# Ten of 22 feature tiles of each FFN for both token halves together, in seven block products for eight

## The chip, the cores and the metric
One core of a Trainium2 chip. The metric is device time in microseconds, the median of some runs. The engines named below are TensorE (PE, with its weight loads as PEld), VectorE (DVE), ScalarE (ACT), GpSimd (POOL) and SyncE (SP), which only issues transfers here.

## What is computed
A block of 1024 tokens of width 1024, all fp32 in and out. The reference, cut to its frame:

```python
x = x + 0.5 * _swiglu(_rms_norm(x, ffn1_norm), ffn1_w_gate, ffn1_w_up, ffn1_w_down)
h = _rms_norm(x, mix_norm)
proj = h @ w_in
...
mixed = concatenate([o_gla, o_rwkv])       # two recurrent mixers over chunks of tokens
x = x + mixed @ w_out
x = x + 0.5 * _swiglu(_rms_norm(x, ffn2_norm), ffn2_w_gate, ffn2_w_up, ffn2_w_down)
return _rms_norm(x, final_norm)
# _swiglu(h, g, u, d) = (silu(h @ g) * (h @ u)) @ d, with 2816 features between
```

## The kernel before
The tokens are worked in two halves A and B of 512 (`HT`). The 2816 features of an FFN are 22 tiles of 128 (`NF`). Each fp32 product is three products of rounded parts: `mm3` (and its yielding form `mm3y`) multiplies high by high, high by low and low by high parts. A weight tile gets its parts in `stage`: SP loads it (`raw`, `NR` buffers), ACT casts the high part `wH` (L394), DVE subtracts it for the low part `wL` (L395). The normalised tokens are kept as the parts `xnH` and `xnL`.

`ffn` is a generator over one half. Feature tiles go in groups of four; for each tile 48 gate and up products into the banks `pgu`, `silu` on ACT, the product `hf` on DVE, its parts `hH` and `hL`; then for each group 24 down products per tile into `pdn`, which DVE adds to x (L533). Every product is a yield, so that other code can take from the generator as many products as it wants. That is what `mixers` does: between the small steps of a mixer (two GLA units, four RWKV pairs: `rwkv_unit`) it writes FFN products of the other half into TensorE's stream, as many as a table of latencies says (`LAT`, `SLACK`, `FILL`). So B's first FFN (`f1b`) fills A's mixer, and A's second (`f2a`) fills B's. TensorE's stream is in the order in which it is written; the other engines' streams are ordered by a scheduler that also moves work of later code ahead.

An RWKV pair first inverts its triangular blocks of 32 by 63 small DVE operations (L89 to L91, n from high to 1; the transposed result is D, L94), then makes `p`, `pav`, and then goes through 8 chunks in turn: `pz` product, Z on DVE (L147), `pz`, UV by DVE and ACT (L152, L153), `pz`, the new state Xn on DVE (L159), with `py` beside it. A group norm over the pair's output YS (L168 to L177), the transposes `pyT`, and two DVE operations end it (L186 to L190), and `YS` is stored to DRAM as `mix`. `outprep` loads the eight mix tiles and makes `xnH`, `xnL` of them (L940, L941); `outproj` is the output projection (`pout`), which DVE adds to x (L953).

After the mixer the main sequence says how many of the FFN's steps are taken where:

```python
mixers(A, f1b)
...
load_x(A, xsp(A))
outprep(A)
run(f1b, n=3)
outproj(A)
run(f1b)
new_xn(A)
norm(A.x, A.XH, A.XL, "n2")
```

`mixers` itself stops taking products at a label, `last=("gu", 5, 20)`, that is at the gate and up products of tile 20 in the last group; `run(f1b, n=3)` stands over the output projection's preparation, and the last `run(f1b)` over the norm.

## Time and profile before
| | |
|---|---|
| runs | 2159.74, 2160.78, 2161.89 us, median 2160.78 |
| span of the profiled execution | 2160.3 us |
| PE busy | 2138.7 us, 99% of the span |
| DVE busy | 1298.8 us, 60% |
| ACT busy | 894.7 us, 41% |
| POOL busy | 83.2 us, 4% |
| mean granted clock of TensorE | 0.999 |

The profiled execution has nothing around its span that the runs' times show: the median lies 0.5 us above it. Busy times are of one engine, and the engines work beside each other, so their sum is no time. A granted clock of 1.00 is 2.4 GHz and 0.5 is 1.2 GHz.

### The profile page before, as it was taken

How to read it: one execution, taken by the hardware profiler on the slowest of the kernel's cores; microseconds unless marked ns; L12 is line 12 of the kernel's file. 1: busy time of each engine (PE TensorE's matmuls, PEld its weight loads, DVE VectorE, ACT ScalarE, POOL GpSimd, SP SyncE). 2: the span in 40 equal slices, each digit the busy share in tenths (PEclk: the TensorE clock that was granted, in tenths of full speed). 3: DMA queues.
4: the chain of work that ended last, by engine and by line, in shares of the span. 5: the costliest groups of instructions: out<-in, count | busy, mean ns of one | idle time of the engine just before them, and what ended most of it. 6: DMA issues, size and time to landing. Idle time of an engine off the chain costs nothing.

```text
span 2160.3 us, 34594 instructions
## 1 busy us (share of the span) xinstructions
PE 2138.7 (99%) x12924; PEld 1682.7 (78%) x12924; DVE 1298.8 (60%) x3387; ACT 894.7 (41%) x1719; POOL 83.2 (4%) x161
## 2 busy tenths in 40 slices
...
GB/s 197 89 86 98 103 94 97 145 193 188 267 102 94 123 99 90 108 92 176 108 126 198 194 271 93 93 118 103 91 106 91 178 88 142 93 98 97 94 95 76
DMA packets 135064, 269.61 MB, mean 125 GB/s; under 512 B 16080, under 2 KB 18160, under 8 KB 134896
## 3 DMA queue, kind: packets, MB, share of 16 engines
...
## 4 chain that ended last, share of the span: by engine, by line
PE 96%; DVE 2%; DMA 1%; ACT 1%; issue 0%; SPq 0%; ACTq 0%; DVEq 0%
PE pgu L43 45%; PE pdn L43 23%; PE pp L43 11%; PE pout L43 4%; PE pz L43 3%; PE pv L43 2%; PE po L43 1%; PE py L43 1%; PE ptn L46 1%; PE pt L46 1%; PE pB L43 1%; PE pg L43 1%; DMA UV<-d_vt 0%; PE pav L43 0%; PE p L43 0%; DVE lb L89 0%
## 5 line engine op out<-in xcount | busy, mean ns | idle before, releaser
L394 ACT CAST wH<-raw 128x512 fp32r<-128x512 f32 (+2 forms) x670 | 413.2, 620 | 882.1 <-PE pgu L43 367.7
L395 DVE TENSOR_TENSOR wL<-raw,wH 128x512 fp32r<-128x512 f32 (+2 forms) x670 | 458.8, 688 | 472.9 <-ACT wH L394 468.2
L43 PE MATMUL pgu<-xnH,wH 128*128 128x512 f32 (+1 forms) x1424 | 563.8, 397 | 0.0
L43 PE MATMUL pgu<-xnL,wH 128*128 128x512 f32 (+1 forms) x1424 | 563.4, 396 | 0.3 <-DVE xnL L479 0.3
L43 PE MATMUL pgu<-xnH,wL 128*128 128x512 f32 (+1 forms) x1424 | 562.5, 395 | 0.2 <-DVE wL L395 0.2
L43 PEld LDWEIGHTS pgu<-xnL,wH 128*128 128x128 f32 x1424 | 267.5, 188 | 59.4 <-DVE xnL L479 0.7
L43 PEld LDWEIGHTS pgu<-xnH,wL 128*128 128x128 f32 x1424 | 267.3, 188 | 59.3 <-DVE wL L395 0.4
L43 PEld LDWEIGHTS pgu<-xnH,wH 128*128 128x128 f32 x1424 | 267.2, 188 | 58.7
L43 PE MATMUL pdn<-wH,hL 128*128 128x512 f32 x704 | 281.6, 400 | 0.0
L43 PE MATMUL pdn<-wH,hH 128*128 128x512 f32 x704 | 280.0, 398 | 0.0
L43 PE MATMUL pdn<-wL,hH 128*128 128x512 f32 x704 | 279.0, 396 | 0.0
L533 DVE SCALAR_TENSOR_TENSOR x<-pdn,x 128x512 f32<-128x512 f32 x192 | 131.9, 689 | 136.1 <-PE pdn L43 135.3
L43 PEld LDWEIGHTS pdn<-wH,hL 128*128 128x128 f32 x704 | 132.1, 188 | 31.1 <-DVE hL L574 0.4
L43 PEld LDWEIGHTS pdn<-wL,hH 128*128 128x128 f32 x704 | 132.2, 188 | 30.5
L43 PEld LDWEIGHTS pdn<-wH,hH 128*128 128x128 f32 x704 | 132.1, 188 | 29.8 <-ACT hH L573 0.5
L43 PE MATMUL pp<-xnH,wH 128*128 128x512 f32 x352 | 140.4, 399 | 0.0
L43 PE MATMUL pp<-xnH,wL 128*128 128x512 f32 x352 | 138.5, 393 | 0.0
L43 PE MATMUL pp<-xnL,wH 128*128 128x512 f32 x352 | 138.4, 393 | 0.0
L570 DVE TENSOR_TENSOR hf<-pgu,silu 128x512 f32<-128x512 f32 x88 | 60.8, 691 | 95.9 <-PE pgu L43 95.5
L43 PEld LDWEIGHTS pp<-xnH,wL 128*128 128x128 f32 x352 | 66.1, 188 | 15.4
L43 PEld LDWEIGHTS pp<-xnH,wH 128*128 128x128 f32 x352 | 66.1, 188 | 15.1 <-issue 0.7
L43 PEld LDWEIGHTS pp<-xnL,wH 128*128 128x128 f32 x352 | 66.2, 188 | 14.3
...
## 6 DMA issues: line engine op xcount, KB each, us to landing
...
d_x<-x SPq DMA_DIRECT2D x8, 512.0 KB, 2.6
d_AR<-AR POOLq DMA_DIRECT2D x8, 512.0 KB, 4.7
...
```

The source lines that it names most:

```text
L43: return self.t.matmul(out,lhsT,rhs,**kw)
L46: return self.t.transpose(out,in_,idn)
L394: S.copy(H, raw)
L395: V.tensor_tensor(L, raw, H.bitcast(F32), op=SUB)
L533: V.scalar_tensor_tensor(h.x[tt][:, co], ps, 0.5, h.x[tt][:, co], op0=MULT, op1=ADD)
L570: V.tensor_tensor(hf, pgu[1], s, op=MULT)
```

## The change
Tiles 12 to 21 of each FFN (five `PAIRS`) leave the generator and are computed for both halves in blocks of two by two: two feature tiles or two halves of the model width on one side, the two token halves on the other, by Winograd's form of Strassen's product: seven block products for eight, with sums of weight blocks and of token blocks ahead and sums of results behind.

`combine` makes the token sums T1 to T4. `joint_up` goes through the pairs; for gate (m=0) and up (m=1) it makes 7 block products of 12 matmuls (`pju`), with three new weight sums `s1`, `s2`, `s3` and a fourth in place on POOL, sums behind them on DVE, and then `put`s seven combinations of the four hidden blocks, each as high and low part in a tile `hh` of 512 KB (two buffers), to DRAM. `joint_down` goes through the seven products in `ORDER`; for each it goes through the five pairs, loads a combination back (`hh`, five buffers), sums weight blocks on POOL and makes 12 matmuls into four banks (`pjd`); behind each product DVE adds the banks to x of both halves. Half B's normalised tokens go through DRAM (`norm_store`, `from_store`); x of both halves is loaded again behind `joint_up`.

The generators keep twelve tiles, in three groups (`FOURS`), in the first FFN's A half in six (`TWOS`). The label in `mixers` is as before, and no group 5 exists in `FOURS`. `NH, NL, NR` go from 8, 8, 3 to 6, 6, 4. The diff, cut:

```diff
-GROUPS = [[0, 1, 2, 3], [4, 5, 6, 7], [8, 9, 10, 11], [12, 13, 14, 15], [16, 17, 18, 19], [20, 21]]
-GROUPS_LAST = [[0, 1], [2, 3, 4, 5], [6, 7, 8, 9], [10, 11, 12, 13], [14, 15, 16, 17], [18, 19, 20, 21]]
+
+NS = 12
+PAIRS = [(f, f + 1) for f in range(NS, NF, 2)]
+FOURS = [list(range(f, min(f + 4, NS))) for f in range(0, NS, 4)]
+TWOS = [list(range(f, min(f + 2, NS))) for f in range(0, NS, 2)]
+CUT = 6
+
+ORDER = [1, 6, 2, 7, 5, 4, 3]
...
-NH, NL, NR = 8, 8, 3
+NH, NL, NR = 6, 6, 4
...
+    def joint_up(w, X, ep):
+
+        def tmp(nm):
+            return ep.tile([P, HT], F32, tag="e", bufs=11, name=nm)
+
+        def left(f1, f2, m):
+
+            raw = {(i, kh): stage_load(wgu[w][(f * 2 + m) * 2 + kh]) for kh in range(2) for i, f in ((1, f1), (2, f2))}
+            yield 1, stage_f(raw[1, 0])
+            s1 = ep.tile([P, HT], F32, tag="s", bufs=3, name="s1")
+            GP.tensor_tensor(s1, raw[2, 0], raw[2, 1], op=ADD)
+            s2 = ep.tile([P, HT], F32, tag="s", bufs=3, name="s2")
+            GP.tensor_tensor(s2, s1, raw[1, 0], op=SUB)
+            yield 6, stage_f(s2)
+            yield 2, stage_f(raw[1, 1])
+            s3 = ep.tile([P, HT], F32, tag="s", bufs=3, name="s3")
+            GP.tensor_tensor(s3, raw[1, 0], raw[2, 0], op=SUB)
+            yield 7, stage_f(s3)
+            yield 5, stage_f(s1)
+            yield 4, stage_f(raw[2, 1])
+            GP.tensor_tensor(s2, raw[1, 1], s2, op=SUB)
+            yield 3, stage_f(s2)
+
+        for j, (f1, f2) in enumerate(PAIRS):
+            gate = {}
+            for m in range(2):
+                C = {}
+                for i, u in left(f1, f2, m):
+                    ps = pm.tile([P, HT], F32, tag="pm", name="pju") if i in (6, 7, 4) else pa.tile([P, HT], F32, tag="pa", name="pju")
+                    for q in range(4):
+                        sl = slice(P * q, P * q + P)
+                        xo = (X[i][0][:, q], X[i][1][:, q])
+                        mm3(ps, (u[0][:, sl], u[1][:, sl]), xo, q == 0, q == 3)
...
+            def put(op, f):
+                hh = ep.tile([P, 2, HT], F32R, tag="hh", bufs=2, name="hh")
+                halved(f, hh[:, 0], hh[:, 1])
+                nc.gpsimd.dma_start(hid_dram(w, j, op), hh.bitcast(F32).rearrange("p a t->p (a t)"))
+
+            put(1, a11)
+            s1 = tmp("s1")
+            GP.tensor_tensor(s1, a21, a22, op=ADD)
+            s2 = tmp("s2")
+            GP.tensor_tensor(s2, s1, a11, op=SUB)
+            put(6, s2)
+            put(2, a12)
+            GP.tensor_tensor(a11, a11, a21, op=SUB)
+            put(7, a11)
+            put(5, s1)
+            put(4, a22)
+            GP.tensor_tensor(s2, a12, s2, op=SUB)
+            put(3, s2)
...
+        for i in ORDER:
+            ps = banks(int(i in (6, 7, 4)))
+            for j in range(n):
+                u = right(i, j)
+                hh = ep.tile([P, 2, HT], F32R, tag="hh", bufs=5, name="hh")
+                nc.sync.dma_start(hh.bitcast(F32).rearrange("p a t->p (a t)"), hid_dram(w, j, i))
+                for t in range(4):
+                    to = slice(P * t, P * t + P)
+                    mm3(ps[t], (hh[:, 0, to], hh[:, 1, to]), u, j == 0, j == n - 1)
...
+    norm_store(B, "n1")
+    run(f1a, until=("dn", 1, 1))
+    tcm = tc.tile_pool(name="tp", bufs=1, side="right", reuse_waits="tile")
+    tpool = tcm.__enter__()
+    fcm, fpool = extras("left")
+    X = combine(A, B, tpool, fpool)
+    fcm.__exit__(None, None, None)
+    run(f1a)
+    spill(A)
+    hp.close()
+    close_x(A)
+    ecm, ep = extras("left")
+    joint_up(0, X, ep)
+    ecm.__exit__(None, None, None)
+    tcm.__exit__(None, None, None)
+    open_x(A)
+    load_x(A, xsp(A))
+    open_half(B, "right")
     load_x(B, xin(B))
-    new_xn(B)
-    norm(B.x, B.XH, B.XL, "n1")
-    run(f1a)
-    f1b = ffn(B, 0)
+    ecm, ep = extras("left")
+    joint_down(0, A, B, ep)
+    ecm.__exit__(None, None, None)
+    from_store(B)
+    B.stored = False
+    hp = Hid("right", 5)
+    f1b = ffn(B, 0, hp)
     new_xn(A)
...
     run(f2a, n=3)
+    to_store(A)
     outproj(B)
...
+    A.stored = True
+    tcm, tpool = extras("left")
+    fcm, fpool = extras("left")
+    hp = Hid("right", 3)
+    f2b = ffn(B, 1, hp, groups=[[f, f + 1] for f in range(0, CUT, 2)])
+    run(f2b, until=("gu", 0, 1))
+    X = combine(B, A, tpool, fpool)
+    fcm.__exit__(None, None, None)
+    run(f2b)
+    spill(B)
+    hp.close()
+    close_x(B)
+    ecm, ep = extras("left")
+    joint_up(1, X, ep)
+    ecm.__exit__(None, None, None)
+    tcm.__exit__(None, None, None)
+    open_x(B)
+    load_x(B, xsp(B))
+    open_x(A)
+    load_x(A, xsp(A))
+    ecm, ep = extras("left")
+    joint_down(1, B, A, ep)
+    ecm.__exit__(None, None, None)
+    hp = Hid("right", 5)
```

How it moves instructions, by the order of both programs. On PE, in a chunk of the last pair of A's mixer, before (`pgu` is a gate or up product of `f1b`):

```order
L43 MATMUL pz<-Z,R_8997 64x64 x2
L43 MATMUL pgu<-xnH,wL 128x512
L43 MATMUL pgu<-xnH,wH 128x512
L43 MATMUL pgu<-xnL,wH 128x512
L43 MATMUL pgu<-xnH,wL 128x512
L43 MATMUL pgu<-xnH,wH 128x512
L43 MATMUL pgu<-xnL,wH 128x512
L43 MATMUL pgu<-xnH,wL 128x512
L43 MATMUL pgu<-xnH,wH 128x512
L43 MATMUL pgu<-xnL,wH 128x512
L43 MATMUL pz<-UV,WN_9025 64x64
L43 MATMUL pz<-UV,WN_9026 64x64
```

Nine FFN products stand there between the `pz` that takes Z and the `pz` that takes UV. In the changed kernel, some chunks earlier (`pdn` is a down product of `f1b`):

```order
L43 MATMUL pdn<-wH,hL 128x512
L43 MATMUL pdn<-wH,hH 128x512
L43 MATMUL pdn<-wL,hH 128x512
L43 MATMUL pdn<-wH,hL 128x512
L43 MATMUL pz<-Z,R_9714 64x64 x2
L43 MATMUL pz<-UV,WN_9740 64x64
L43 MATMUL pz<-UV,WN_9741 64x64
L43 MATMUL pz<-Xn,AR 64x64 x2
L43 MATMUL py<-Xn,AR 64x64 x2
L43 MATMUL py<-UV,W_8699 64x64
L43 MATMUL py<-UV,W_8700 64x64
```

The four `pdn` rows are the last FFN products of this mixer: the 174 mixer products behind them, this chunk and all later ones, have none between them.

At the end of the mixer, before, on PE (`pyT` are the transposes behind the last group norm):

```order
L43 MATMUL pgu<-xnL,wH 128x512
L43 MATMUL pgu<-xnH,wL 128x512
L43 MATMUL pgu<-xnH,wH 128x512
L46 MATMUL pyT<-ct,YS 128x128 x4
L43 MATMUL pgu<-xnL,wH 128x512
L43 MATMUL pgu<-xnH,wL 128x512
L43 MATMUL pgu<-xnH,wH 128x512
L43 MATMUL pgu<-xnL,wH 128x512
```

and in the changed kernel, there:

```order
L43 MATMUL py<-Xn,AR 64x64 x2
L43 MATMUL py<-UV,W_9938 64x64
L43 MATMUL py<-UV,W_9939 64x64
L46 MATMUL pyT<-ct,YS 128x128 x4
L43 MATMUL pout_10733<-wH,xnH 128x512
L43 MATMUL pout_10733<-wL,xnH 128x512
L43 MATMUL pout_10733<-wH,xnL 128x512
```

Before, 128 FFN products stand between `pyT` and `pout`; now the first `pout` product is the next row.

On SP, where FFN1 goes from `joint_up` to `joint_down` in the changed kernel (`xnL` is B's tokens, `x` half A's, `hh` a combination of hidden blocks, `raw` a weight tile; the waits name a queue or an engine: DMASW is a queue of POOL, DMAHW one of SP):

```order
L662 DMA xnL_4701<-d_xf1_705 128x512 [waits DMAHW6_49]
L548 DMA x_3803<-d_x_0_2083 128x1024 [waits DMAHW7_49,DVE_49]
...
L548 DMA x_3809<-d_x_0_2083 128x1024 [waits DMAHW2_49]
L815 DMA hh_3846<-d_hid0_0_1_2396 128x1024 [waits DMASW5_49,DMASW7_49,DMASW3_49,DMAHW3_49,DMASW1_49,DMASW0_49]
L815 DMA hh_3866<-d_hid0_1_1_2737 128x1024 [waits DMAHW4_49]
...
L815 DMA hh_3926<-d_hid0_4_1_3760 128x1024 [waits DMAHW7_49,DMASW4_49]
L393 DMA raw_3978<-in_wdn1_dram 128x512 [waits DMAHW0_49,Pool_49]
L815 DMA hh_3961<-d_hid0_0_6_2405 128x1024 [waits DMAHW3_49,DMAHW1_49,PE_49]
```

Every load of `joint_down` behind its first weight tiles stands behind the four loads of x, which wait for DVE, and behind the first `hh`, which waits for four of POOL's stores.

On ACT at the same place (`hh` casts are the puts of the last pair; `xnH` casts belong to `from_store`):

```order
L633 CAST hh_3766<-s2_3764 128x512 [waits DMASW3_49,Pool_49]
L633 CAST hh_3771<-u3_3545 128x512 [waits DMASW4_49,DVE_49,Activation_49]
L633 CAST hh_3777<-p1_3482 128x512 [waits DMASW5_49,DVE_49,Pool_49]
L633 CAST xnH_4698<-xnL_4700 128x512 [waits DMAHW7_49,PE_49]
L633 CAST hh_3782<-s1_3762 128x512 [waits DMASW6_49,DVE_49]
L633 CAST xnH_4698<-xnL_4700 128x512 [waits DMAHW0_49]
L633 CAST xnH_4698<-xnL_4700 128x512 [waits DMAHW1_49]
L633 CAST xnH_4698<-xnL_4700 128x512 [waits DMAHW2_49]
L633 CAST xnH_4699<-xnL_4701 128x512 [waits DMAHW3_49]
L633 CAST hh_3787<-c22_3564 128x512 [waits DMASW7_49,DVE_49]
```

The casts of the puts wait in turn for POOL's stores (DMASW), whose tile they take, so that the last ones come after them all.

In FFN2's joint_down the loads on SP stand thus (`x_20290` is half A's, `x_20273` half B's):

```order
L548 DMA x_20290<-d_x_0_2083 128x1024
L815 DMA hh_20313<-d_hid1_0_1_18866 128x1024 [waits DMAHW7_49,DMASW7_49]
...
L815 DMA hh_20393<-d_hid1_4_1_20230 128x1024 [waits DMAHW3_49,DMASW3_49]
L393 DMA raw_20445<-in_wdn2_dram 128x512 [waits DMAHW4_49,Pool_49]
L815 DMA hh_20428<-d_hid1_0_6_18875 128x1024 [waits DMAHW5_49,DMAHW7_49,DMASW0_49,PE_49]
L393 DMA raw_20448<-in_wdn2_dram 128x512 [waits DMAHW6_49]
L815 DMA hh_20455<-d_hid1_1_6_19216 128x1024 [waits DMAHW0_49,DMASW7_49,PE_49]
L548 DMA x_20273<-d_x_1_11334 128x1024 [waits DMASW5_49,DMASW7_49,DMASW1_49,DVE_49]
L548 DMA x_20275<-d_x_1_11334 128x1024 [waits DMAHW1_49]
...
L393 DMA raw_20475<-in_wdn2_dram 128x512 [waits DMAHW6_49]
L815 DMA hh_20482<-d_hid1_2_6_19557 128x1024 [waits DMAHW7_49,PE_49]
```

Here the first `hh` waits for data alone, and half B's x, which waits for stores of POOL and for DVE, stands between the second and the third `hh` of product 6.

## Rows read from the trace of the kernel before

**Rows 1.** The page, parts 1 and 4: TensorE, and the last chain by engine.
```profile
PE 2138.7 (99%) x12924; PEld 1682.7 (78%) x12924; DVE 1298.8 (60%) x3387; ACT 894.7 (41%) x1719; POOL 83.2 (4%) x161
...
PE 96%; DVE 2%; DMA 1%; ACT 1%; issue 0%; SPq 0%; ACTq 0%; DVEq 0%
```

**Rows 2.** The last chain in time: start, length, engine, products of one kind.
```profile
163.43 44.40 PE pgu L43 x192
207.83 22.23 PE pdn L43 x96
```

**Rows 3.** Windows: length, busy us (count) of PE, PEld, DVE, ACT, POOL; clock; DMA; GB/s.
```profile
844.20:986.10 141.90, 141.90 (x848) 105.61 (x845) 77.32 (x226) 49.95 (x107) 0.00 (x0) 1.00 0.33 99
986.10:1015.50 29.40, 29.40 (x129) 23.84 (x128) 17.64 (x28) 13.15 (x24) 0.00 (x0) 1.00 0.64 224
1060.20:1082.30 22.10, 22.10 (x97) 17.64 (x96) 17.34 (x57) 9.26 (x18) 0.00 (x0) 1.00 0.38 137
427.00:432.00 5.00, 5.00 (x27) 4.54 (x27) 1.16 (x2) 4.33 (x8) 3.48 (x7) 0.66 0.91 326
7.00:12.00 5.00, 4.30 (x20) 3.69 (x20) 3.92 (x11) 3.59 (x11) 0.00 (x0) 1.00 0.99 365
```

**Rows 4.** Timeline of DVE (start, us, line, operation): inverse of pair 3.
```profile
844.72 0.33 DVE L91 TENSOR_TENSOR R<-R,lb 128x168 f32<-128x168 f32 x1
...
870.51 0.45 DVE L94 STREAM_TRANSPOSE D<-R 128x256 f32<-128x256 f32 x1
```

**Rows 5.** Timeline of PE: pair 3's first products, and one of a chunk.
```profile
880.09 0.69 PE L43 MATMUL p<-D,WA 32*32 32x32 f32 x32
...
883.82 1.15 PE L43 MATMUL pav<-UV,WA 64*64 64x64 f32 x32
...
937.77 0.33 PE L43 MATMUL pz<-Z,R 64*64 64x64 f32 x4
```

**Rows 6.** Timeline of DVE: one chunk of pair 3, then its group norm's ends.
```profile
935.23 0.23 DVE L147 TENSOR_TENSOR Z<-pz,AV 128x64 f32<-128x64 f32 x1 [0.93 <-PE pz L43]
...
938.15 0.22 DVE L152 COPY UV<-pz 64x64 f32<-64x64 f32 x1 [0.51 <-PE pz L43]
...
940.80 0.28 DVE L159 SCALAR_TENSOR_TENSOR Xn<-pz,pc,XP 128x64 f32<-128x64 f32 x1
...
949.48 0.69 DVE L168 TENSOR_REDUCE sm<-YS 128x8 f32<-128x512 f32 x1 [0.31 <-ACT YS L142]
...
956.32 0.69 DVE L177 TENSOR_TENSOR YS<-YS,vr 128x512 f32<-128x512 f32 x1
```

**Rows 7.** Timeline of ACT: a chunk, the last YS, the first output projection operand.
```profile
938.40 0.21 ACT L153 COPY UV<-pz 64x64 f32<-64x64 f32 x1 [2.17 <-DVE UV L152]
...
986.14 2.29 ACT L186 ACTIVATE YS<-pyT,vt 64x256 f32<-64x256 f32 x4 [0.94 <-PE pyT L46]
...
1001.83 0.62 ACT L940 CAST xnH<-xnL 128x512 fp32r<-128x512 f32 x1 [6.93 <-DMA xnL<-d_mix]
```

**Rows 8.** Timeline of DVE behind the output projection: first and last of the norm.
```profile
1058.68 2.48 DVE L953 TENSOR_TENSOR x<-pout,x 128x512 f32<-128x512 f32 x4
...
1069.09 0.75 DVE L459 TENSOR_SCALAR xs<-x,rs 128x1024 f32<-128x1024 f32 x1
```

**Rows 9.** The page, parts 5 and 6: staging, store, load.
```profile
L394 ACT CAST wH<-raw 128x512 fp32r<-128x512 f32 (+2 forms) x670 | 413.2, 620 | 882.1 <-PE pgu L43 367.7
L395 DVE TENSOR_TENSOR wL<-raw,wH 128x512 fp32r<-128x512 f32 (+2 forms) x670 | 458.8, 688 | 472.9 <-ACT wH L394 468.2
...
d_AR<-AR POOLq DMA_DIRECT2D x8, 512.0 KB, 4.7
...
AR<-d_AR SPq DMA_DIRECT2D x8, 512.0 KB, 5.0
```

**Rows 10.** Lines of POOL: its costliest operation that is no DMA.
```profile
L217 POOL MEMSET sc<- 128x1024 f32 x4 | 3.8, 959 | 126.7 <-PE po L43 122.9 <-PE pp L43 3.9
```

More of the change, by code (lines that the diff above doesn't have):

```diff
@@ L446, in rstd, with norm, put, norm_store @@
         return xs, rs
-    def norm(xts, XH, XL, gain, table=False, mid=None):
+    def norm(h, gain, table=False, mid=None):
         with tc.tile_pool(name="np", bufs=1, side="left", reuse_waits="tile") as npool:
             g.np = npool
-            norm_(xts, XH, XL, gain, table, mid)
-    def norm_(xts, XH, XL, gain, table, mid):
+            def put(kt, o, pv):
+                S.mul(h.xh(kt)[:, o], pv, vec(gain, kt))
+                V.scalar_tensor_tensor(h.xl(kt)[:, o], pv, vec(gain, kt), h.xh(kt)[:, o].bitcast(F32), op0=MULT, op1=SUB)
+            norm_(h.x, put, table, mid)
+    def norm_store(h, gain):
+        with tc.tile_pool(name="np", bufs=1, side="left", reuse_waits="tile") as npool:
+            g.np = npool
+            xts = []
+            for i in range(4):
+                t = npool.tile([P, D], F32, tag="x", bufs=4, name="x")
+                nc.sync.dma_start(t, xin(h)(i))
+                xts.append(t)
+            def put(kt, o, pv):
+                f = npool.tile([P, 256], F32, tag="f", bufs=4, name="f")
+                S.mul(f, pv, vec(gain, kt))
+                nc.gpsimd.dma_start(xf(h, kt)[:, o], f)
+            norm_(xts, put, False, None)
+    def xf(h, kt):
+        return dram(f"xf{h.i}", [P, 8 * HT])[:, HT * kt:HT * kt + HT]
+    def norm_(xts, put, table, mid):
         def scaled(tp):
@@ L490, in open_half, with open_x @@
         h.pool = h.cm.__enter__()
[L491 removed]
+        open_x(h)
+    def open_x(h):
+        h.xcm = tc.tile_pool(name=f"x{h.i}", bufs=1, side=h.side, reuse_waits="tile")
         h.xpool = h.xcm.__enter__()
@@ L500, in new_xn @@
     def new_xn(h):
-        h.XH = h.pool.tile([P, 8, HT], F32R, tag="xnH", name="xnH")
-        h.XL = h.pool.tile([P, 8, HT], F32R, tag="xnL", name="xnL")
+        h.XH, h.XL = [[h.pool.tile([P, 4, HT], F32R, tag=f"xn{n}{i}", name=f"xn{n}") for i in range(2)] for n in "HL"]
     def load_x(h, src, mid=None):
@@ L584, in ffn, with __init__, close, halved @@
         yield from down(len(groups) - 1, old)
+    class Hid:
+        def __init__(self, side, n):
+            self.cm = tc.tile_pool(name="hid", bufs=1, side=side, reuse_waits="tile")
+            self.pool, self.n = self.cm.__enter__(), n
+            self.tile = self.pool.tile
+        def close(self):
+            self.cm.__exit__(None, None, None)
+    def halved(f, H, L):
+        S.copy(H, f)
+        V.tensor_tensor(L, f, H.bitcast(F32), op=SUB)
+    def stage_f(f):
+        H = wk.tile([P, VW], F32R, tag="wH", bufs=NH, name="wH")[:, :HT]
+        L = wk.tile([P, VW], F32R, tag="wL", bufs=NL, name="wL")[:, :HT]
+        halved(f, H, L)
+        return H, L
@@ new lines, in whole, with to_store, from_store @@
+    def whole(h, kt, pool):
+        t = pool.tile([P, HT], F32, tag="f", bufs=4, name="xw")
+        if h.stored:
+            nc.sync.dma_start(t, xf(h, kt))
+        else:
+            GP.tensor_tensor(t, h.xh(kt).bitcast(F32), h.xl(kt).bitcast(F32), op=ADD)
+        return t
+    def to_store(h):
+        for kt in range(8):
+            t = t2("xs")
+            GP.tensor_tensor(t, h.xh(kt).bitcast(F32), h.xl(kt).bitcast(F32), op=ADD)
+            nc.gpsimd.dma_start(xf(h, kt), t)
+    def from_store(h):
+        new_xn(h)
+        for kt in range(8):
+            raw = h.xl(kt).bitcast(F32)
+            nc.sync.dma_start(raw, xf(h, kt))
+            halved(raw, h.xh(kt), h.xl(kt))
@@ new lines, in combine, with new @@
+    def combine(c1, c2, tp, fp):
+        def new(nm):
+            return [tp.tile([P, 4, HT], F32R, tag=f"{nm}{n}", name=nm) for n in "HL"]
+        T1, T2, T3, T4 = [new(f"T{i}") for i in range(1, 5)]
+        b22 = new("b22") if c2.stored else (c2.XH[1], c2.XL[1])
+        for q in range(4):
+            b11, b12, b21, b22f = whole(c1, q, fp), whole(c2, q, fp), whole(c1, q + 4, fp), whole(c2, q + 4, fp)
+            if c2.stored:
+                halved(b22f, b22[0][:, q], b22[1][:, q])
+            t1 = fp.tile([P, HT], F32, tag="t", bufs=3, name="t1")
+            GP.tensor_tensor(t1, b12, b11, op=SUB)
+            halved(t1, T1[0][:, q], T1[1][:, q])
+            t3 = fp.tile([P, HT], F32, tag="t", bufs=3, name="t3")
+            V.tensor_tensor(t3, b22f, b12, op=SUB)
+            halved(t3, T3[0][:, q], T3[1][:, q])
+            t2_ = fp.tile([P, HT], F32, tag="t", bufs=3, name="t2")
+            GP.tensor_tensor(t2_, b22f, t1, op=SUB)
+            halved(t2_, T2[0][:, q], T2[1][:, q])
+            V.tensor_tensor(t2_, t2_, b21, op=SUB)
+            halved(t2_, T4[0][:, q], T4[1][:, q])
+        return {1: (c1.XH[0], c1.XL[0]), 2: (c1.XH[1], c1.XL[1]), 3: b22, 4: T4, 5: T1, 6: T2, 7: T3}
```

156 lines of the change are left out of this document (126 added, 30 removed).

## The prediction
> **What bounds the kernel now.** I read the page first: TensorE is busy for 2138.7 of 2160.3 us and holds 96% of the chain that ended last [rows 1]. So before is a queue of products without holes, and its time is the products' time plus about 21 us. Then the pieces of that chain: gate/up products come 192 in 44.40 us and down products 96 in 22.23 us, 231 ns each whatever they are [rows 2]. Then the windows, to see how the mixers, whose own products are tiny and wait for each other, come to be dense: in the last 141.9 us of A's mixer, in the 29.4 us behind it and in the 22.1 us after the output projection TensorE is busy for the whole stretch [rows 3], because FFN products stand between the mixer's. This is what the reader is to keep: **the FFN's products are the work and also the cover of every wait in the mixers.** A change that removes products and cover must be summed as TensorE's work saved less TensorE's new idle time.
>
> **What is removed.** The order has 10,812 TensorE matmuls before and 10,452 after. Per FFN the ten joint tiles take 840 gate/up products for 960 and 420 down products for 480: 180 fewer, 360 in all, × 231.3 ns = **−83.3 us**. That is certain as far as the pitch holds.
>
> **The mixers lose their cover.** The fillers are now 12 tiles of 22. In the order they run out inside each mixer: after the last one stand 174 mixer products (3.6 chunks of head pair 2; the 32-row products, `pav` and 8 chunks of pair 3; two transposes `pyT`), then `pout`. Before, that place of A's mixer is 844.2 to 986.1 us [rows 3]. What the stretch takes unfilled goes by its chain. DVE is at step n=20 of pair 3's 32-row inverse there (844.72) and reaches D at 870.51 [rows 4], 26 us later, with FFN work between; the same rows back to back would take 12.6, but pair 2's group norm (4), four late wL and the chunks share DVE. I take 23 (18.5 to 26). From D through `p`, `pav` (880.09 to 883.82 + 1.15) and its copy: 5.5 [rows 5]. A chunk is a ring of pz .33, Z .23, pz, UV .22 on DVE and .21 on ACT behind it, pz, Xn .28 [rows 5, 6, 7]: 1.9 us of instructions and six hand-overs of 0.05 to 0.2; with small matmuls at either clock 2.5 to 3.2, I take 2.8; eight are 22.4. The group norm runs from 949.48 to 957.0 with three wL in it, 5.7 without [rows 6]; `pyT` 0.6. Sum 57 us, of which TensorE is busy about 21 (a chunk's products 1.46 packed, × 11.6, and the rest): **36 idle per mixer** (29 to 43).
>
> Behind `pyT`, YS is evacuated at 986.14 and the first cast of the output projection's operand stands at 1001.83, released by its load [rows 7]. In between lie the sum, the store of mix7, four x loads and the load, all in one SP queue, unchanged. Before, 128 down and gate/up products cover this [rows 3]; after, nothing: **14 per mixer** (11 to 17). Behind `pout` the norm goes from 1058.68 (x) to the last scaled tile at 1069.09 + .75 [rows 8], then transposes and evacuation; its first part overlaps `pout`: **9 per mixer** (7 to 11). Two mixers: 2 × (36 + 14 + 9) = **118**.
>
> **joint_up to joint_down.** Every pair ends with seven puts through two tiles `hh`: cast .62 (L394's form), subtraction .69 (L395's), a 512 KB store by POOL's queue 4.7 (`d_AR`) [rows 9]. Between pairs the scheduler lays them beside the next pair's 38.9 us of products (168 × .2313), so they cost nothing; 7 puts by two tiles need about 22. Behind the last pair there is no cover. From the last product T0: evacuation and the product with the gate 1.4, two POOL sums 2.2, cast and subtraction 1.3, landed at 9.6; the tile's next user, put 7, at 15.6, and put 4 at 22 with hand-overs. In FFN1 joint_down's first feature load sits on joint_up's tile and waits for that very put (by the built program's semaphore values), behind x loads that wait for the last subtraction, at 18; it takes 5.0 (`AR<-d_AR`) [rows 9]. Queued behind it on SP is every load of joint_down. **T1 27.5** (20, with the put at half its duration, to 33). In FFN2 the tiles lie elsewhere: only four x(A) loads go ahead, a stall of 8; but x(B)'s loads stand in SP before op 6's third feature load and wait for the last put (24), so 10.5 more once the products of op 1 and two of op 6 are used up. **T2 18.5** (10 to 24).
>
> **The smaller ones.** POOL's two-input sums stand in no row of before. They must take more than DVE's .69 [rows 9]; a MEMSET writes 1024 columns in .959 [rows 10], so 512 with two reads and a write may be 3 × .48 = 1.44. I take 1.1, in the middle. A pair in joint_up then has 39 DVE operations × .69 = 26.9, 12 sums (13.2) and 7 store issues on POOL beside 38.9 of TensorE: two columns that fit, if they overlap. I take 5 for ten pairs (0 to 12: not overlapped they are 40.1). The first weight sum of each joint_up: 2 × 2. joint_down moves 35 × 512 KB and 55 × 256 KB in 97.1 us, 337 GB/s; before shows 365 at share .99 [rows 3]; 5 for both (0 to 20). f1b's first tile after joint_down 3. After a pause in `pz` products the granted clock fell to half for about 3.4 us once (0.66 in 427 to 432) [rows 3], a loss of 1.7; after seven resumptions 2 each, **14** (5 to 20). Norm of B through DRAM, combine's sums, x's spill and reload lie beside f1a's twelve tiles, 200 us of products (12 × 72 × .2313): 0; without that cover the loads, sums and casts would cost some 30.
>
> **Sum.** New idle: 118 + 27.5 + 18.5 + 5 + 4 + 5 + 3 + 14 = 195; −83.3 + 195 = +112. 2160.3 + 112 = **2272 us**; the profiled execution's span is 0.5 below the median shown, which changes nothing. All low ends together give 132 idle, 2209; the high ends 2340 when they do not all come together.
>
> **Rivals.**
> *DVE and POOL take turns in joint_up.* If a sum costs 1.44 and DVE stands still for each, a pair is 26.9 + 17.3 = 44.2 against 38.9: ten pairs 53 us more, 2325; at 1.1 it is 12, which is in my bounds. For it: 25 of the 39 DVE operations read two SBUF tiles while POOL does. Against: the order lets POOL run a product ahead. Chance 0.13. The Trainium skill, "SBUF — State Buffer", section "SBUF: two separate sides", says that a DVE operation with two SBUF inputs and a GpSimd operation that reads SBUF exclude each other for the whole instruction; no row of before can show it, and it would give this rival. The skill's "GPSIMD Engine Reference", section "Performance versus the Vector engine", gives 4497 ns for a sum of 2048 columns, so an estimate of 1.12 us for 512, by which the sum stays 2272.
>
> *joint_down is bound by DMA.* At 300 GB/s instead of 365, 32.8 MB take 109 us for 97: 12 per FFN, and the shuttle of 512 KB writes behind it: 2290 to 2300. For it: a 512 KB load took 5.0 us to land in before, and op 6 wants one with three weight tiles every 2.78 us. Against: 365 was reached with loads that TensorE waited for. Chance 0.10.
>
> *The tails are cheap.* In the unfilled stretch DVE and ACT lose the FFN's casts, and the chunk's ring shrinks to its packed 1.46 with D at 18: T falls to 41 (18 + 5.5 + 11.7 + 5.7 + .6), idle 20 per mixer, 2240; with load and norm at their low ends 2230. Against: the ring's hand-overs are there without any cast. Chance 0.12.
>
> *Faster.* One mechanism could do it: the mixers' waits vanish, because what holds `pz`, the loads and the norm in before is TensorE's own queue and not their chain. Place: the stretch 844 to 1082 without fillers. Price: the whole 118. It decides only when the idle time is under 3 us per mixer with the other terms as they are, or 22 per mixer with all of them at their low ends. Against it: D's chain alone is 18.5, and the 6.93 us of idle for the xnL load [rows 7] does not come from TensorE. Chance 0.05.
>
> **How the numbers follow.** The forecast 0.60, cheap tails 0.12, turns 0.13, DMA 0.10, faster 0.05. The range 2205 to 2345 leaves out the faster side, the upper end of turns with everything else high, and some of the cheapest tails, together under 0.2. A measurement of this kernel tells about 0.2% (4.3 us) from no change. Faster 0.05, same 0.01, slower 0.94.
>
> **What would show it.** In the profile after: TensorE busy about 2055 us and a busy share near 90%; in both mixers a last stretch of some 57 us in which only pz, py, p and pav run with idle before each named by DVE or ACT; some 14 us of idle before the first `pout`, ended by the cast of xnH, itself released by the mix load; idle of 25 to 30 before the first `pjd` of FFN1, ended by DMA hh, and two shorter ones in FFN2; matmuls of joint_up 231 ns apart. I am wrong if joint_up shows idle before each product, ended by POOL or DVE, or joint_down idle before each `pjd`; if the tails stand dense; or if the clock stays low long after the pauses.

## The result and the profile after

The changed kernel takes 2315.45 us against 2160.87, a ratio of 1.071 (95% interval 1.0693 to 1.0727): slower by 154.6 us, inside the range and 43 us above the forecast of 2272. Its runs were 2311.81, 2313.01, 2317.88 and 3588.43 us; the median is that of all four, and the last, a disturbed run, is left out of the ratio. The profiled execution below spans 2316.1 us, 155.8 more than before's.

The page of the changed kernel, parts 1, 2 and 4, answers to [rows 1]: busy time of each engine, TensorE and its granted clock in 40 slices of 57.9 us, and the chain by engine.

```profile
PE 2108.5 (91%) x12564; PEld 1660.0 (72%) x12564; DVE 1516.9 (65%) x3607; ACT 928.0 (40%) x1795; POOL 436.2 (19%) x465
...
PE   8999999498999999994899999999569899978898
...
PEclk9999999799999999995899999999579999989999
...
PE 58%; DVE 9%; DMA 5%; issue 4%; POOL 3%; ACT 2%; SPq 0%; POOLq 0%; DVEq 0%; ACTq 0%
```

TensorE is busy 2108.5 us instead of 2138.7. With 360 products fewer at the old pitch it would be 2055.4, so its work takes 53.1 us longer, much of it at half clock; its idle time grows from 21.6 to 207.6 us. Its share of the chain that ended last has fallen from 96% to 58%. The slices below 9 show where: slices 8 to 10 and 36 to 38 hold the two passages from `joint_up` to `joint_down`, 19 to 20 and 29 to 30 the two mixer ends, 32 `combine` in FFN2; the clock is lowest in 8, 19, 29 and 30, then in 20 and 36.

What TensorE waited for in the changed kernel (line, releaser, total us, times, longest):

```profile
PE pjd L43 <- DMA hh<-d_hid: 46.1, 3, 32.7
PE pout L43 <- ACT xnH L1202: 27.1, 2, 13.6
PE pz L43 <- ACT UV L153: 17.7, 24, 2.1
...
PE pjd L43 <- DVE wL L634: 13.6, 6, 6.2
PE pyT L46 <- DVE YS L177: 13.3, 2, 6.6
```

The reader is to see three kinds: `joint_down` waiting for hidden blocks and weight parts, the output projection for its operand, and `pz` and `pyT` of the mixers for ACT and DVE. Of these only `pz` waits in before, for 1.8 us.

Windows of the changed kernel, columns as in [rows 3]. The first is A's mixer from its first `pg` product to `pout`, the next two its filled and its unfilled part; then `joint_up`, the stall and `joint_down` of FFN1, and stall and `joint_down` of FFN2.

```profile
770.70:1104.20 333.50, 288.85 (x2882) 210.47 (x2881) 241.35 (x937) 131.68 (x289) 0.95 (x1) 0.89 0.33 110
770.70:1030.00 259.30, 257.74 (x2536) 188.23 (x2535) 207.63 (x773) 111.70 (x232) 0.95 (x1) 0.99 0.34 112
1030.00:1104.20 74.20, 31.10 (x349) 22.25 (x347) 33.72 (x165) 19.98 (x57) 0.00 (x0) 0.53 0.30 104
229.10:425.60 196.50, 195.25 (x841) 157.68 (x839) 146.74 (x193) 75.77 (x133) 94.20 (x84) 1.00 0.40 140
425.60:458.20 32.60, 0.00 (x0) 0.00 (x0) 11.27 (x18) 8.39 (x15) 10.86 (x12) 0.57 0.90 331
458.20:570.90 112.70, 105.30 (x421) 83.92 (x422) 55.02 (x77) 23.45 (x39) 33.02 (x23) 0.93 0.80 281
...
2068.70:2081.20 12.50, 0.05 (x1) 0.00 (x0) 8.99 (x10) 1.76 (x3) 8.78 (x8) 0.62 0.87 319
2081.20:2205.10 123.90, 106.03 (x420) 83.78 (x421) 53.17 (x81) 25.52 (x42) 34.49 (x28) 0.91 0.83 297
```

The filled part is as dense as before [rows 3]: 257.7 of 259.3 us. The unfilled part has 31.1 us of TensorE in 74.2, at a mean clock of 0.53. `joint_up` takes 196.5 us (196.6 in FFN2) for 840 products, 194.3 at the pitch, at full clock. The stalls are 32.6 and 12.5 us, and `joint_down` takes 112.7 and 123.9 us for products of 97.1.

**Where 155.8 us come from.** I cut the executions at TensorE's landmarks and take from each stretch its products at the pitch of 231.3 ns, or the time that before had for the same work. A's region, from the last `pjd` (570.9) to the end of the norm behind `pout` (1163.9), takes 593.0; before took 701.3 for it (385.5 to 1086.8), less 720 products that moved out, 166.5: 58.2 more. The passages, last `pju` to last `pjd`, take 145.3 and 136.4 for 97.1. The generators up to `joint_up` reach it at 229.1, where before's time less the moved tiles is 385.5 - 166.5 = 219.0; in FFN2 they take 111.6 for 99.9. The end, from 2205.1, takes 111.0 for 99.9 and before's 6.7. What is left is B's region.

| stretch | measured us more than its work before | forecast |
|---|---|---|
| A's mixer with load and norm | 58.2 | 59 and some 6 of clock and start |
| B's mixer with load and norm (the rest) | 62.8 | 59 and some 4 of clock |
| FFN1, `joint_up` end to `joint_down` end | 48.2 | 27.5 + 2.5 and 3 of clock |
| FFN2, the same | 39.3 | 18.5 + 2.5 and 3 of clock |
| two `joint_up` | 4.5 | 9 |
| generators beside `combine` | 10.1 + 11.7 | 0 |
| end of the program | 4.4 | 0 |
| products saved | -83.3 | -83.3 |

The mixer's end goes as forecast almost step by step. On DVE in the unfilled part of A's mixer (timeline; start, length, line, operation):

```profile
1050.67 0.45 DVE L94 STREAM_TRANSPOSE D<-R 128x256 f32<-128x256 f32 x1
...
1056.79 0.23 DVE L147 TENSOR_TENSOR Z<-pz,AV 128x64 f32<-128x64 f32 x1 [4.69 <-ACT AV L130]
...
1083.37 0.69 DVE L168 TENSOR_REDUCE sm<-YS 128x8 f32<-128x512 f32 x1 [0.71 <-ACT YS L142]
```

The last FFN product ends at 1031.9. D stands at 1050.67, 19 us later (forecast 23, its low end 18.5), the first Z of the last pair at 1056.79, the next at 1059.62 and then one every 3.0 us (forecast 2.8) but for one gap of 5.6 us, in which the evacuation of pair 2's transposes (2.28 us on ACT, from 1067.31) stands ahead of the chunk's UV. So the eight chunks, up to the last state at 1082.65, take 25.9 us for 22.4. The group norm of the last pair runs from 1083.37 on, to 1089.57 (6.2 for 5.7). On ACT the end of it and the load behind it:

```profile
1090.84 2.28 ACT L186 ACTIVATE YS<-pyT,vt 64x256 f32<-64x256 f32 x4 [5.14 <-PE pyT L46]
1103.60 1.98 ACT L1202 CAST xnH<-xnL 128x512 fp32r<-128x512 f32 x3 [10.48 <-DMA xnL<-d_mix]
```

`pyT` is evacuated at 1090.84, and the first operand of the output projection is cast at 1103.60, released by its load, 12.8 us later (15.7 with cover in [rows 7]). TensorE waits 13.5 us for it.

Of the passage in FFN1, where the last `joint_up` product ends at 425.4, the transfers that SP issued:

```profile
425.46 1.95 SPq L548 DMA_DIRECT2D x<-in_x_dram  x4
427.51 6.88 SPq L662 DMA_DIRECT2D xnL<-d_xf  x8
447.42 1.81 SPq L548 DMA_DIRECT2D x<-d_x  x4
```

The chain there:

```profile
432.48 8.68 DMA d_hid<-hh
449.46 8.66 DMA hh<-d_hid
```

The page, part 6, for these transfers (count, KB each, median us to landing):

```profile
d_hid<-hh POOLq DMA_DIRECT2D x70, 512.0 KB, 3.2
hh<-d_hid SPq DMA_DIRECT2D x70, 512.0 KB, 5.3
```

SP's queue has x of B and eight loads of B's tokens (`xnL`) at 425.46 to 434; x of A is issued only at 447.42, when the last subtraction of the puts is done; the feature loads follow it at 449.46, and TensorE starts at 458.3. The store in the chain takes 8.68 us and the load 8.66, where the medians are 3.2 and 5.3; 4 MB of loads move beside the one and 2 MB of x beside the other, and the window has DMA at 0.90.

### The profile page after: what moved, and what is told of

It reads as the page before. It is cut to its first block, busy times and chain, and to the rows that moved or that the text cites. A ratio compares the mean times of both kernels' runs of the same rounds, so it can differ in the third digit from the quotient of the medians.

```text
span 2316.1 us, 34996 instructions
## 1 busy us (share of the span) xinstructions
PE 2108.5 (91%) x12564; PEld 1660.0 (72%) x12564; DVE 1516.9 (65%) x3607; ACT 928.0 (40%) x1795; POOL 436.2 (19%) x465
## 4 chain that ended last, share of the span: by engine, by line
PE 58%; DVE 9%; DMA 5%; issue 4%; POOL 3%; ACT 2%; SPq 0%; POOLq 0%; DVEq 0%; ACTq 0%
PE pgu L43 16%; PE pp L43 11%; PE pdn L43 9%; PE pjd L43 5%; PE pout L43 4%; PE pz L43 3%; PE pv L43 2%; DMA raw<-in_wdn_dram 2%; PE pju L43 2%; DMA d_hid<-hh 1%; PE py L43 1%; PE po L43 1%; DVE x L821 1%; PE pt L46 1%; DVE wL L634 1%
## 5 line engine op out<-in xcount | busy, mean ns | idle before, releaser
L401 DVE TENSOR_TENSOR wL<-raw,wH 128x512 fp32r<-128x512 f32 (+1 forms) x430 | 300.4, 705 | 283.9 <-ACT wH L400 283.3
L400 ACT CAST wH<-raw 128x512 fp32r<-128x512 f32 (+1 forms) x430 | 263.7, 618 | 456.0 <-PE pgu L43 170.2
L43 PE MATMUL pgu<-xnL,wH 128*128 128x512 f32 (+1 forms) x784 | 312.5, 399 | 0.0
L43 PE MATMUL pgu<-xnH,wH 128*128 128x512 f32 (+1 forms) x784 | 312.2, 399 | 0.0
L43 PE MATMUL pgu<-xnH,wL 128*128 128x512 f32 (+1 forms) x784 | 310.9, 397 | 0.1
L43 PE MATMUL pjd<-wH,hh 128*128 128x512 f32 x560 | 186.3, 413 | 56.8 <-DMA hh<-d_hid 46.1
L43 PE MATMUL pju<-T,wH 128*128 128x512 f32 x640 | 200.7, 395 | 2.4 <-ACT wH L633 2.4
L43 PEld LDWEIGHTS pgu<-xnH,wH 128*128 128x128 f32 x784 | 148.7, 190 | 32.7 <-ACT xnH L459 0.2
L43 PE MATMUL pdn<-wH,hH 128*128 128x512 f32 x384 | 154.9, 405 | 9.7 <-DVE hf L606 3.8
L43 PE MATMUL pdn<-wH,hL 128*128 128x512 f32 x384 | 155.8, 406 | 0.0
L43 PE MATMUL pju<-T,wL 128*128 128x512 f32 x320 | 126.1, 394 | 0.0
```

The source lines that it names most:

```text
L43: return self.t.matmul(out,lhsT,rhs,**kw)
L400: S.copy(H, raw)
L401: V.tensor_tensor(L, raw, H.bitcast(F32), op=SUB)
```

## The experiments

All kernels start from the changed one (2311.8 to 2317.9 us); a single run that differs by less than 6 us shows nothing in its total, and then the stretch is read.

**1. e9_cover: the cover given back.** Both generators that fill the mixers run all 22 tiles again:

```diff
-    f1b = ffn(B, 0, hp)
+    f1b = ffn(B, 0, hp, groups=[list(range(f, min(f + 4, NF))) for f in range(0, NF, 4)])
...
-    f2a = ffn(A, 1, hp)
+    f2a = ffn(A, 1, hp, groups=[list(range(f, min(f + 4, NF))) for f in range(0, NF, 4)])
```

Expected: 

> Gives the mixers their cover back and changes nothing else: B's first FFN and A's second run all 22 tiles again as fillers, though ten of them are made jointly too, so that their products count twice in x. That adds 2 x 720 products, 333 us at the pitch. By the cover theory the idle of the mixers, of the output projection's load and of the norm (122 us with the clock) goes: 2316 + 333 - 122 = 2527 us (2515 to 2540). If that idle had another cause, such as the smaller staging buffers or the split tokens, it stays: 2649 us.

Measured: 2527.28 us. The window of A's mixer up to `pout`, for this kernel:

```profile
767.40:1196.90 429.50, 427.98 (x3507) 316.59 (x3507) 301.63 (x1028) 176.18 (x365) 0.95 (x1) 1.00 0.36 113
```

It is 429.5 us long with 427.98 busy, as before's 586.1 to 1015.6 was: 1440 products (333 us) cost 212. The idle time of the mixers is the missing cover and nothing else; staging buffers and split tokens have no part in it.

**2. e2_spread and e10_slack: the same cover, placed otherwise.**

```diff
-SLACK = 1.490
-FILL = 0.549
+SLACK = 0.8          # e2_spread
+FILL = 0.3
...
-        last = ("gu", 5, 20)
+        last = ("gu", 2, 10)
...
-    run(f1b, n=3)
+    run(f1b, n=2)
```

(f2a likewise; e10_slack has SLACK 1.2, FILL 0 and nothing else.)

Expected of e2_spread: 

> The same twelve tiles as cover, but spread: the table's factors SLACK 1.49 and FILL 0.549 become 0.8 and 0.3, so that fewer FFN products go to each wait, and 144 are kept back: 96 over the output projection's preparation and 48 over the norm. By my theory (lost cover, where it runs out) the 13.5 us before the output projection, the 4.9 behind it and most of the tail of 54 us go, and some idle appears inside the chunks: 2316 less 2 x 45 = 2226 us (2190 to 2260). By the rival that the mixers are bound by their own chain, so that spreading only moves the idle into the chunks, only the load and the norm come back: 2316 less 2 x 19 = 2278 us (2265 to 2295).

Expected of e10_slack: 

> The twelve tiles as cover with the table's SLACK 1.2 and FILL 0 (1.49 and 0.549 before; 0.8 and 0.3 in e2_spread), nothing kept back, so that the fillers end 30 mixer products before the mixer's end instead of 174. If the waits that the table covers are about 1.2 times its latencies or less, the tail's 54 us of idle fall to about 15 and nothing appears ahead of it: 2316 - 2 x 35 = 2246 us (2235 to 2270). If the waits need the full 1.49, idle appears between the chunks, the clock falls there as in e2_spread, and the time stays at 2300 us or more.

Measured: 2324.73 us median (2315.64 to 2333.49, ratio to before 1.0761, interval 1.0723 to 1.0799) and 2327.47 us. My expectation failed in both: nothing was gained. A's mixer to `pout` in e2_spread, with a piece of it, and in e10_slack:

```profile
771.20:1113.30 342.10, 311.94 (x2848) 216.78 (x2849) 233.19 (x933) 134.10 (x292) 0.95 (x1) 0.87 0.30 101
...
946.00:984.00 38.00, 37.15 (x278) 24.80 (x277) 14.64 (x55) 11.03 (x27) 0.00 (x0) 0.51 0.27 89
```

```profile
771.00:1107.40 336.40, 294.03 (x2888) 211.85 (x2888) 237.06 (x940) 132.27 (x290) 0.95 (x1) 0.92 0.34 112
```

With 703 and 743 FFN products in it, it lasts 342.1 and 336.4 us, with 737 in the changed kernel 333.5. In e2_spread the output projection and the norm are covered and TensorE is busier (311.9 us for 288.9), but at a mean clock of 0.87: short pauses all along the mixer, and half clock in whole stretches with hardly a pause in them (37.15 of 38.0 us busy at 0.51 from 946 on), so that the products there lose what the tail gains. From 984 to `pout` the clock is at 1.00 again. In e10_slack TensorE is idle for 42.4 us of the window instead of 44.7. Both came out as their rivals had it or worse: the place of the cover hardly matters here; its amount does. How fast the mixers could go with fillers placed by a better table than these three, I have not tried.

**3. e6_ns18: four joint tiles instead of ten.** `NS = 18`, and the last generator's groups cut to fit.

Expected: 

> Four joint tiles per FFN instead of ten (NS = 18, two pairs). Saved: 4/10 of 83.3 = 33 us. By the cover theory the fillers now run out close to the mixer's end: the tail's 54 us of idle per mixer falls to about 10 and 14, and load and norm stay bare: 2 x 33 = 66; the fixed costs stay: stalls of 33 and 13 us before the first pjd, some 12 of joint_down, 22 of combine. 2160.9 - 33 + 66 + 46 + 12 + 22 = 2274 us (2255 to 2290). If all cost went with the number of joint tiles, as 155 us do for ten: 2160.9 + 62 = 2223 us or less.

Measured: 2289.77 us, the upper end of what the cover theory gave, and far from 2223. A's mixer and the two passages with `joint_down` in it:

```profile
689.80:1092.40 402.60, 384.14 (x3315) 280.56 (x3314) 284.30 (x1002) 160.03 (x338) 0.95 (x1) 0.99 0.37 116
409.80:489.90 80.10, 44.03 (x173) 34.29 (x172) 47.16 (x74) 19.35 (x35) 21.90 (x20) 0.79 0.74 261
2004.70:2077.30 72.60, 47.60 (x172) 36.84 (x172) 43.26 (x65) 14.45 (x25) 20.46 (x19) 0.84 0.72 258
```

The mixer has 384.1 of 402.6 us busy, so most of its cover is back. But the passages, with 38.9 us of products each, take 80.1 and 72.6 us: 41 and 34 more than their products, where ten tiles have 48 and 39. The cost of the passage is nearly fixed.

**4. e5_ns22: no joint tile at all, the rest kept.** `NS = 22`; `joint_down` returns at once.

Expected: 

> No joint tiles: all 22 tiles of both FFNs in the generators again (NS = 22), with everything else of the change kept: six, six and four staging buffers, the split tokens, norm of B through DRAM, the sums of combine, x stored and loaded again. If the cost lies in the lost cover and in the joint stages, only combine's 10 and 12 us in the two generators and an uncovered reload of x and tokens before B's first FFN are left: 2160.9 + 22 + 10 = 2193 us (2180 to 2205). If the smaller staging buffers are what slows the change, idle appears before pgu and pdn everywhere and it is 2230 us or more; if the rewriting costs nothing, 2165.

Measured: 2203.56 us against 2159.28 for a run of before beside it: 44 us, just inside the expectation. The largest waits of TensorE behind the start of the program:

```profile
PE pdn L43 <- DVE x L569: 5.0, 3, 4.1
PE pdn L43 <- ACT silu L603: 3.8, 2, 3.5
PE pgu L43 <- DVE x L569: 3.1, 1, 3.1
```

None is for weight parts, for which TensorE waits 2.2 us in all, so the smaller staging buffers are not the cause; the waits shown lie in the generators beside `combine`. The rest I have located only by halves: A's output projection ends at 1079.6 (1060.0 before), B's at 1784.0 (1760.3), so 20 us lie ahead of the one, 4 between, and the rest behind.

**5. e8_nocombine: combine left out.**

```diff
-    X = combine(A, B, tpool, fpool)
+    X = {i: (A.XH[i % 2], A.XL[i % 2]) for i in range(1, 8)}
```

Expected: 

> Leaves out combine, its token loads and its sums (joint_up multiplies untransformed tokens in their place), in both FFNs. The generators around it, f1a and the first half of f2b, took 10.1 and 11.7 us longer than their products. If combine's work on DVE, ACT and POOL delays the hidden features there, 15 of these 22 go: 2301 us (2296 to 2306). If the groups of two tiles or B's norm through DRAM cost this, less than 6 go: 2310 us or more.

Measured: 2299.62 us. The two generator stretches in this kernel, and then in the changed kernel:

```profile
21.00:224.50 203.50, 201.31 (x899) 163.73 (x897) 106.20 (x194) 73.05 (x131) 10.41 (x18) 0.99 0.41 131
1750.60:1852.50 101.90, 101.03 (x435) 81.44 (x434) 48.47 (x76) 30.49 (x53) 5.50 (x4) 1.00 0.31 98
```

```profile
20.40:229.10 208.70, 202.84 (x899) 162.90 (x898) 131.91 (x214) 79.45 (x143) 34.29 (x34) 0.99 0.38 123
1760.50:1872.10 111.60, 104.49 (x435) 82.87 (x434) 75.66 (x101) 38.86 (x70) 24.97 (x16) 0.95 0.30 99
```

203.5 us for 208.7 and 101.9 for 111.6: 14.9, as expected; the other 6.9 of the 21.8 us no run places. DVE is busy 48.5 us instead of 75.7 in the second stretch, POOL 5.5 instead of 25.0, and the clock stays at 1.00. combine is not hidden by the products around it. The longest wait there in the changed kernel, 3.3 us before a `pdn`, is for `silu`, which stands on ACT behind a cast of a token sum (1801.31), and that cast had waited 2.07 us for POOL.

**6. e4_nosums: weight sums of joint_down left out**, with the 20 loads per FFN that only they need.

```diff
         def right(i, j):
-            ...
+            return stage_f(get(j, int(i == 3))(int(i in (2, 3))))
```

Expected: 

> Leaves out the weight sums of joint_down (products 6, 7, 5 and 4 take one loaded block in their place), so 35 weight tiles are loaded per FFN instead of 55 and POOL does nothing there. If the staging chain of load, POOL sum, cast and subtraction is what makes joint_down 15.5 and 26.7 us longer than its products behind the first stall, about 25 us go: 2291 us (2284 to 2300). If DVE's additions to x, the loads of hidden blocks or the clock behind the pauses do it, less than 8 go: 2308 us or more.

Measured: 2290.39 us. `joint_down` behind the first stall, in FFN1 and FFN2:

```profile
459.50:559.30 99.80, 99.78 (x420) 80.83 (x421) 48.15 (x77) 23.94 (x39) 0.00 (x0) 0.97 0.80 262
2069.10:2178.10 109.00, 103.66 (x420) 83.18 (x421) 50.65 (x81) 25.14 (x42) 2.17 (x4) 0.94 0.83 291
```

99.8 and 109.0 us instead of 112.7 and 123.9. The expectation held: the weight path of `joint_down` costs 28 us for both, and the total fell by 25. The first stalls hardly changed (33.9 and 13.0 us for 32.7 and 12.6).

**7. e11_order: product 2 ahead of product 6.** `ORDER = [1, 2, 6, 7, 5, 4, 3]`, with the banks taken in turn.

Expected: 

> joint_down takes its products in the order 1, 2, 6, 7, 5, 4, 3 instead of 1, 6, 2, 7, 5, 4, 3, so that the sums of product 6 (three weight tiles and two POOL sums for each pair) have 13.9 us of products more to be made in. If the staging chain is what makes joint_down long, as e4_nosums says, 5 to 8 us go in each FFN: 2303 us (2298 to 2308). If the loads as such are the limit, nothing changes: 2316.

Measured: 2322.18 us. `joint_down` takes 115.1 and 123.2 us: no gain. So more lead for POOL's sums is not what was lacking. Whether e4_nosums gained by the missing sums or by the missing 5 MB of loads per FFN, these runs do not separate; in the changed kernel DMA is at 0.80 and 0.83 of its time there. The trace of the changed kernel points to the loads. In `joint_down` of FFN1, ACT's casts wait mostly for POOL's sums, and the sums mostly for weight loads (ACT's and POOL's waits there, the longest of each):

```profile
ACT wH L633 <- POOL t2f L796: 27.7, 4, 17.9
...
POOL t2f L795 <- DMA raw<-in_wdn_dram: 20.6, 4, 13.1
POOL t L791 <- DMA raw<-in_wdn_dram: 19.7, 5, 12.0
```

**8. e3_right, e3_late, e7_xl: what the first stall waits for.**

```diff
-    ecm, ep = extras("left")
+    ecm, ep = extras("right")                  # e3_right
     joint_down(0, A, B, ep)
...
+            if i == 1:                          # e3_late, e7_xl: in joint_down
+                for h, src in loads:
+                    load_x(h, src)
...
-        E = [ep.tile(...) for t in range(4)]
-        Gs = [ep.tile(...) for t in range(4)]
+            eg = [c2.pool.tile([P, 4, HT], F32R, tag=f"xnL{i}", name="EG") for i in (1, 0)]   # e7_xl, FFN1
```

Expected of e3_right: 

> In FFN1 the tiles of joint_down lie where the token sums lay, so that the first feature load no longer waits for a store of joint_up; its place in SP's queue stays behind the four loads of x, which wait for the last subtraction. If the stall of 32.7 us is the wait for the tile, as my prediction had it, the stall falls by 10 or more: 2306 us or less. If it is the place in SP's queue behind x, nothing changes: 2316 us, within 4.

Expected of e3_late: 

> As the run before it, and in both FFNs the loads of x are written behind the first product of joint_down, which puts the five feature loads of that product ahead of half A's x in SP's queue. If SP's order is the cause, the stall before FFN1's first product falls from 32.7 to about 15 us and FFN2's from 12.6 to about 5, part of which comes back before product 6: 2298 us (2290 to 2306). If the transfers themselves are the limit, the same idle stands before product 6: 2312 us or more.

Expected of e7_xl: 

> As e3_late, and in FFN1 the results E and G of joint_down lie where B's reloaded tokens xnL will lie, so that these eight loads (2 MB) and their casts can't be moved ahead of the puts. If this traffic, with its casts between the puts on ACT, is what lengthened the stall in FFN1, the stall falls from 19.3 us in e3_late to 8 or less, and the time by 10 to 15 against e3_late: 2294 us (2288 to 2299). If the chain of puts alone sets it, the stall stays at 15 to 20: 2304 us or more.

Measured: 2309.81, 2306.88 and 2307.45 us. The windows of FFN1's stall and `joint_down` for e3_right, e3_late and e7_xl, a fence each:

```profile
425.10:458.50 33.40, 0.27 (x3) 0.06 (x1) 11.96 (x19) 8.38 (x15) 10.86 (x12) 0.56 0.88 327
458.50:566.30 107.80, 102.16 (x421) 81.54 (x422) 54.10 (x77) 23.64 (x39) 33.68 (x23) 0.96 0.84 294
```

```profile
425.30:444.90 19.60, 0.27 (x2) 0.07 (x1) 7.30 (x12) 4.97 (x9) 7.27 (x8) 0.59 0.96 351
444.90:565.60 120.70, 106.63 (x421) 83.54 (x422) 57.58 (x85) 27.48 (x45) 35.75 (x27) 0.91 0.83 296
```

```profile
425.80:431.80 6.00, 0.23 (x2) 0.07 (x1) 5.21 (x4) 0.62 (x1) 4.64 (x4) 0.76 0.92 295
431.80:559.90 128.10, 107.21 (x421) 84.49 (x422) 61.38 (x88) 32.25 (x54) 36.83 (x32) 0.89 0.88 313
```

Two of the totals lie between what the two sides of their expectations gave (2309.81 and 2306.88), so the stages decide. In e3_right the stall stays at 33.4 us although the first feature load no longer waits for a store: it is the place in SP's queue behind x, not the tile. In e3_late the stall is 19.6 where 15 was expected (and 6.7 in FFN2 for 5), and in e7_xl, where the eight token loads can't run ahead, 6.0. But `joint_down` behind it grows from 112.7 to 120.7 and 128.1. Stall and stage together are 141.2 in e3_right, 140.3 in e3_late and 134.1 in e7_xl; the kernels that leave this passage alone show 139.8 (e8_nocombine) to 145.5. So of 27 us that the stall loses in e7_xl, some 6 to 11 stay, and in the other two nothing that can be told. The rest turns into waits behind it, of which the largest in e7_xl's FFN1, 12.6 us in all, are for casts of weight parts. e7_xl's stall came out as the theory had it, its total as the rival: the stall can be moved, and most of it comes back. e8_nocombine points the same way in FFN2, where its stall is 31.4 us and `joint_down` 108.6 instead of 12.5 and 123.9.

**9. e12_all: late loads, slack and order together.**

Expected: 

> The edits of e3_late, e10_slack and e11_order together. If they are independent, their gains add: by my expectations 2316 - 10 - 70 - 12 = 2224 us (2210 to 2260), which is still slower than before. By the rival of e10_slack 2290 us or more.

Measured: 2322.97 us (2319.2 to 2333.01; ratio to before 1.0745, interval 1.0725 to 1.0764). Nothing is left of the sum of gains, since two of its three parts have none alone. No run points to a version that beats before.

## Why the prediction was right, and where it was off

**The products.** 360 fewer at 231 ns: the matmul counts are 12924 and 12564, and `joint_up` runs at 196.5 us for 194.3. Right.

**The mixers lose their cover.** The term that decides. Forecast 59 per mixer and 10 for clock and start, measured 121.0 for both. Inside it D came at 19 us for 23, the eight chunks took 25.9 for 22.4, the group norm 6.2 for 5.7, the load 13.5 for 14, and behind the first `pout` TensorE is idle 5.0 us for 9. Of the 58.2 us of A, 46.9 are idle time (50.5 after 3.6) and 11.3 are products that take longer. e9_cover shows the cause. My rivals "cheap tails" and "faster" fell with it: the chunk's ring did not shrink when the casts of the FFN were gone.

**joint_up to joint_down, and joint_down's DMA.** Right in kind, under-sized: 27.5 + 18.5 + 5 and some 6 of clock make 57, measured 87.5. T1, the stall in FFN1, came out inside its bounds, 32.7 for 27.5. I took the price of a put and of a feature load from rows of another stage ([rows 9], 4.7 and 5.0); in the passage the chain shows 8.68 and 8.66, with 4 MB and 2 MB of loads beside them, half of the first moved ahead by the scheduler. So x could be issued only 22 us behind the last product where I had 18, and the load behind it took 3.7 longer. And "waits for that very put" was true in the program and not what ended last: e3_right takes that wait away and the stall stays, since the loads of x stand ahead in SP's queue. T2 held, with 12.6 for 8 and 9.0 for 10.5: half B's x is issued at 2100.50, when the last store has landed, and TensorE then waits 9.0 us for what stands behind it in SP's queue, a weight load issued at 2102.90 that takes 7.39, and not the third feature load. The term that was far off is the stage itself. I gave `joint_down` itself 5 us for both FFNs; it has 15.6 (112.7 - 97.1) and 26.8 (123.9 - 97.1) behind the first stalls, of which I had put 10.5 under T2. In FFN1 8.2 of it are products that take longer (105.3 us busy) and 7.3 waits for weight parts; in FFN2 8.9 and 17.9, T2's 9.0 among them. The rival "bound by DMA" comes nearer to that, at 12 per FFN; e4_nosums and e11_order only show that it is the weight path, and the waits there speak for the loads.

**Norm, combine, spill at 0.** Wrong: 21.8 us. The step that failed is "lie beside f1a's twelve tiles". The products do cover TensorE's side, but combine's operations go into the same DVE, ACT and POOL queues as the FFN's own, ahead of `silu` and `hf`, and in the first half of f2b there are only 100 us of cover.

**DVE and POOL take turns.** The sums on POOL cost more than the 1.1 that I took:

```profile
L712 POOL TENSOR_TENSOR s<-raw,s 128x512 f32<-128x512 f32 x20 | 32.8, 1641 | 15.9 <-DVE wL L634 15.9
```

By line, the weight sums of `joint_up` take 1.34 to 1.64 us on the mean, 1.25 to 1.27 at 427 to 433 us where DVE had little to do, and DVE's own subtractions 1.01 (`wL`) and 1.56 (`hh`) instead of .69. The timeline shows which operations are held up (POOL, then DVE, in `joint_up`):

```profile
276.19 1.75 POOL L702 TENSOR_TENSOR s<-raw 128x512 f32<-128x512 f32 x1
278.02 1.63 POOL L704 TENSOR_TENSOR s<-s,raw 128x512 f32<-128x512 f32 x1
...
276.71 1.78 DVE L634 TENSOR_TENSOR hh<-u,hh 128x512 fp32r<-128x512 f32 x1
278.41 0.68 DVE L730 TENSOR_TENSOR u<-pju,p 128x512 f32<-128x512 f32 x1
```

The subtraction of two SBUF tiles takes 1.78 us; the operation at 278.41, which reads a bank of `pju`, takes 0.68 inside a sum of POOL. That agrees with the rule in the Trainium skill, "SBUF — State Buffer", section "SBUF: two separate sides". The estimate of 1.12 us from the Trainium skill's "GPSIMD Engine Reference", section "Performance versus the Vector engine", was below all of these sums. But POOL is busy 94.2 and DVE 146.7 of 196.5 us there, and `joint_up` still runs at TensorE's pitch. As the bound of that stage the rival is refuted.

**Clock.** By size, the term that failed most. The mean granted clock is 0.941 after 0.999: some 270 us at half clock (0.059 x 2316 x 2), where I had priced seven short resumptions at 14 us, and a busy TensorE at about 2055 us as a sign of being right. It is busy for 53.1 us more. The rest of the change is idle time: 186.0 us more than before (207.6 after 21.6), where the forecast's waits without the clock add up to 181. So the waits are right in their sum, and that is in part luck: the mixers' were too high and those of `joint_down` and `combine` too low. 39 of the 43 us above the forecast are products that take longer. Not all 53.1 need be the clock's: in the unfilled part of A's mixer TensorE is busy for 31.1 us at a mean clock of 0.53 where I had reckoned 21, and products that stand alone there also count in full.
